# Seven-product order, standard parts ahead of the pair, and a late first gate chunk in a two-layer encoder

## The chip, the cores and the metric

The kernel runs on one core of one Trainium2 chip. The time is the device time of one execution in microseconds (us), the median of several runs. TensorE multiplies, VectorE and ScalarE work on tiles in SBUF and PSUM, GpSimd does a little, and SyncE issues the loads. In the rows PE is TensorE (PEld its weight loads), DVE is VectorE, ACT is ScalarE, POOL is GpSimd and SP is SyncE.

## What is computed

The reference is an encoder trunk over 256 positions of 2048 channels in f32, two layers deep. The change touches what stands at the end of each layer:

```
h = rms_norm(x, mlp_norm[i])
x = x + jnp.square(jax.nn.relu(h @ mlp_w1[i])) @ mlp_w2[i]      # 2048 -> 8192 -> 2048
g = jax.nn.sigmoid(rms_norm(x, ple_norm[i]) @ ple_w_gate[i])    # 2048 -> 2048
x = x + g * (p[i] @ ple_w_proj[i])
```

## The kernel before, in words

**Exact f32 from three passes.** Every operand of TensorE is held as two tiles, a high part (ScalarE's copy into fp32r) and a low part (VectorE's source minus high part). A product is three passes: high by high, high by low, low by high. So each weight tile of 128 x 2048 is loaded into one of four `raw` buffers (L86, DMA on SyncE), copied by ScalarE (L105) and subtracted by VectorE (L106) into one of four `hl` buffers. `Weights.run_ahead` (L118) issues loads and splits at most three tiles ahead of the one TensorE asks for with `ws.next()`; an `hl` buffer is free again when TensorE has used the tile four places earlier.

**The squared-ReLU mixer.** `mlp` (L556) goes over 16 blocks q of 512 hidden channels, two at a time (f = 0..7). `w1(q)` (L568) makes one block: four weight tiles, each 16 matmuls of 512 columns (L580) and 16 of 256 (L585), then ScalarE and VectorE turn the PSUM result into `h` and into four sums of its quarter blocks, `g`. `w2(f, n)` (L615) is a standard part: two weight tiles, 48 matmuls (L345), output columns n (512 of the 2048), added to x at L366. For the output columns n = 0 and 1 `pair(f)` (L621) uses seven products in place of eight for a matrix of 2 x 2 blocks: for each of the two blocks q of the pair seven products of six matmuls (L641). With x and y as the weight tiles of n = 0 and n = 1, each cut into a first and a second half (x0, xq, y0, yq), the products use: 1 x0, 2 xq, 3 yq, 5 x0 + y0, 6 x0 + y0 + yq, 7 y0 + yq, 4 x0 + y0 + yq + xq. VectorE makes the sums in place in the raw tile (L102), so a sum must come after the splits that read the old value, and the split after a sum needs it complete: first VectorE's sum, then ScalarE's copy, then VectorE's subtraction. `add_seven` (L69) puts two products into each `hl` tile: seven tiles for the two blocks of a pair.

**PSUM.** Three buffers of 1024 columns serve `w1`, `w2` and the pair's tiles a (products 1, 5), b (2, 3) and c (7, 6); tile d (product 4) is one of two buffers of 512 columns, which it shares with the transposes. After the second block, VectorE adds each finished tile to x or to `sums` (L649, L655, L657).

**The layer's order** (L674 to L690) is `w1(0)`, `w1(1)`, then for each f: `w1(2f+2)`, `w2(f,2)`, `pair(f)`, `w1(2f+3)`, `w2(f,3)`. At f = 7 there is no further `w1`; behind the pair stand `pair_end` (L659), which combines `sums` into x, and `w2(7,3)`. `after.chunk(c)` (L317) takes the squares of chunk c of x at once and puts its transposes, scaling and split off by four steps (`tick`). The gate that follows (`embed`, L692) multiplies chunks 0, 1, 2, 3 of the normed x by its weights.

**Who sets the order.** The instructions of TensorE and SyncE stand in the order of the program. Those of VectorE, ScalarE and GpSimd are ordered by the scheduler of the language; `tc.high_priority` moves some forward. Each engine then runs its list in order.

Of the kernel before, what the change touches and what calls it, by code (L numbers as in the profile page):

```python
# [15 lines left out]
ALU = mybir.AluOpType  # L16
# [14 lines left out]
RAW_BUFS = 4  # L31
RSQRT_MAGIC = float(0x5F3759DF)
# [10 lines left out]
class Weights:  # L43

# [24 lines left out]
    def add_seven(self, tiles):  # L69


        q, parts = 1024, []
        for x, y in tiles:
# [21 lines left out]
    def divide(self, after_first=None):  # L95
# [3 lines left out]
        for i, (what, (r, c), other, w) in enumerate(steps):  # L99
# [6 lines left out]
            getattr(self.nc, lo).tensor_tensor(hl[:, 1, to], src, hl[:, 0, to].bitcast(F32), ALU.subtract)  # L106
# [32 lines left out]
def encoder(ctx: ExitStack, tc: tile.TileContext, a, out: bass.AP):  # L139
# [35 lines left out]
    def add_mlp(i):  # L175
        def w1(q):
            for c in range(4):
                ws.add(a["mlp_w1"][i, q, c])
# [10 lines left out]
        for f in range(8):  # L189
            if f < 7:  # L190
                w1(2 * f + 2)
            w2(f, 2)
            pair(f)
            if f < 7:
                w1(2 * f + 3)
            w2(f, 3)
# [84 lines left out]
    class Norm:  # L281
# [35 lines left out]
        def chunk(self, c):  # L317
# [9 lines left out]
            put_off(lambda: self.scale(c, turned))  # L327
# [228 lines left out]
    def mlp(i, norm, after):  # L556
# [64 lines left out]
        def pair(f):  # L621


            p15, p76, p23 = psum_mm(f"ps_s{i}_{f}a"), None, psum_mm(f"ps_s{i}_{f}b")
            p4 = sm_pool.tile([P, 512], F32, tag="sm", name=f"ps_s{i}_{f}d")
            k = 0
            for q in (2 * f, 2 * f + 1):
                h, g = hidden[q], forms[q]
                for what in range(7):
                    if k % 2 == 0:  # L630
                        w = ws.next()
                    if what == 4 and p76 is None:
                        p76 = psum_mm(f"ps_s{i}_{f}c")
                    out_ps = (lambda: p15[:, :512], lambda: p23[:, :512], lambda: p23[:, 512:], lambda: p15[:, 512:],
                              lambda: p76[:, :512], lambda: p76[:, 512:], lambda: p4)[what]()
                    for kt in range(2):
                        for m, (s, j) in enumerate(PASSES_W_MOVES):
                            act = (h[:, s, kt, :P], h[:, s, 2 + kt, :P], g[:, s, 3, kt], g[:, s, 0, kt],
                                   g[:, s, 2, kt], g[:, s, 1, kt], h[:, s, 2 + kt, P:])[what]
                            col = (k % 2) * 1024 + kt * 512  # L640
                            nc.tensor.matmul(out_ps, lhsT=act, rhs=w[:, j, col:col + 512],  # L641
# [4 lines left out]
                    if q % 2 == 0:  # L646
                        continue
                    if what == 2:
                        nc.vector.tensor_tensor(x[:, 0, :1024], p23, x[:, 0, :1024], ALU.add)  # L649
                    elif what in (3, 5):  # L650
                        ps, to = (p15, sums[:, :1024]) if what == 3 else (p76, sums[:, 1024:])
                        if f == 0:
                            nc.scalar.activation(to, ps, AF.Copy)
                        else:
                            nc.vector.tensor_tensor(to, ps, to, ALU.add)  # L655
                    elif what == 6:
                        nc.vector.tensor_tensor(x[:, 1, :512], p4, x[:, 1, :512], ALU.add)  # L657

        def pair_end():  # L659
# [7 lines left out]
            after.chunk(0)  # L667
# [4 lines left out]
            after.chunk(1)  # L672
# [4 lines left out]
        for f in range(8):  # L677
# [3 lines left out]
            if f == 7:  # L681
                after.chunk(2)
            pair(f)
            if f == 7:
                pair_end()
            else:
                w1(2 * f + 3)
            w2(f, 3)
            if f == 7:
                after.chunk(3)  # L690
# [242 lines left out]
```

## Time and profile before

| | us |
|---|---|
| median of 3 runs (2074.29 to 2076.41) | 2075.16 |
| the profiled execution, its own time | 2070.65 |
| its span, first to last instruction | 2068.9 |
| PE busy | 1977.0 |
| DVE busy | 1564.3 |
| ACT busy | 1039.6 |

The profiled execution is a run of its own; its time is 1.75 us more than its span. Busy times are unions of instruction times, and those of TensorE overlap, so its busy share says little of how well it is fed. Whether it waits is read from the start times of its matmuls.

### The profile page before, as it was taken

The page shows a single profiled execution, that of the slowest core. Times are in us where ns is not written, and L with a number is a line of the kernel's source. Part 1 is how long each engine was busy: PE and PEld are TensorE (multiplying, and loading weights), DVE is VectorE, ACT ScalarE, POOL GpSimd, SP SyncE. Part 2 cuts the span into 40 slices and gives each one's busy share as a digit, 9 for nine tenths or more (in the row PEclk, how much of TensorE's full clock was granted, in tenths as well). Part 3 has the DMA queues.
Part 4 walks back from the last instruction along what each step waited for, and adds up shares of the span by engine and source line. Part 5 has one row for each costly group of instructions (what it writes and reads, how often), then busy time and mean ns, then how long its engine had stood idle before and what let it go on. Part 6 is the DMA issues. An engine that isn't in the chain of part 4 may idle for free.

```text
span 2068.9 us, 24040 instructions
## 1 busy us (share of the span) xinstructions
PE 1977.0 (96%) x9730; PEld 1668.3 (81%) x9730; DVE 1564.3 (76%) x1771; ACT 1039.6 (50%) x1087; POOL 128.9 (6%) x65
## 2 busy tenths in 40 slices
PE   8999999999999999998999999999999999999798
PEld 6888887878787787877789888787787878788686
DVE  7888768687787868779556567787868778787854
ACT  6345555445444545455454455545545445554543
POOL 3874000000000000000001000000000000000000
PEclk9999999999999999999999999999999999999999
DMA  8545554554536454464453554536364454635542
GB/s 330 192 170 191 206 188 168 187 203 143 224 140 227 152 214 183 143 223 162 152 183 135 183 183 146 224 139 240 137 231 169 159 209 146 222 135 203 182 164 108
DMA packets 55664, 377.43 MB, mean 182 GB/s; under 512 B 6384, under 2 KB 6528, under 8 KB 11648
## 3 DMA queue, kind: packets, MB, share of 16 engines
q1 hardware_dynamic: 55152, 374.82, 49.7%
q8 instruction: 76, 1.25, 0.2%
q10 hardware_dynamic: 144, 1.05, 0.1%
q14 instruction: 36, 0.29, 0.0%
q0 software_dynamic: 256, 0.02, 0.0%
HBM read 373.75 MB, written 2.10 MB: 182 GB/s over the span
## 4 chain that ended last, share of the span: by engine, by line
PE 69%; DVE 27%; issue 2%; ACT 2%; DMA 0%; ACTq 0%; SPq 0%
PE ps_h L580 21%; DVE hl L106 14%; PE ps_h L585 11%; PE ps_o L345 9%; PE ps_g L345 8%; DVE raw L102 7%; PE ps_od L345 4%; PE ps_in L345 4%; PE ps_out L345 3%; PE ps_pool L345 2%; ACT hl L105 2%; PE ps_outp L345 1%; PE ps_e L345 1%; DVE h L600 1%; DVE g L612 1%
## 5 line engine op out<-in xcount | busy, mean ns | idle before, releaser
L105 ACT ACTIVATE hl<-raw 128x2048 fp32r<-128x2048 f32 (+2 forms) x529 | 774.7, 1491 | 769.0 <-PE ps_h L585 315.8
L106 DVE TENSOR_TENSOR hl<-raw,hl 128x2048 fp32r<-128x2048 f32 (+3 forms) x501 | 865.5, 1744 | 381.5 <-ACT hl L105 379.8
L580 PE MATMUL ps_h<-xT_mlp,hl 128*128 128x512 f32 x2048 | 503.6, 399 | 0.0
L580 PEld LDWEIGHTS ps_h<-xT_mlp,hl 128*128 128x128 f32 x2048 | 391.1, 194 | 80.4
L345 PE MATMUL ps_o<-hl,h 128*128 128x512 f32 x1536 | 356.3, 391 | 0.0
L345 PEld LDWEIGHTS ps_o<-hl,h 128*128 128x128 f32 x1536 | 288.0, 189 | 58.7
L585 PEld LDWEIGHTS ps_h<-xT_mlp,hl 128*128 128x128 f32 x2048 | 262.6, 191 | 10.0
L585 PE MATMUL ps_h<-xT_mlp,hl 128*128 128x256 f32 x2048 | 266.0, 283 | 0.0
L345 PE MATMUL ps_g<-hl,xT_ple 128*128 128x512 f32 (+1 forms) x816 | 177.6, 377 | 0.0
L345 PEld LDWEIGHTS ps_g<-hl,xT_ple 128*128 128x128 f32 x816 | 146.4, 188 | 28.2 <-DVE hl L106 0.4
L106 POOL TENSOR_TENSOR hl<-raw,hl 128x2048 fp32r<-128x2048 f32 (+1 forms) x28 | 120.8, 4328 | 55.8 <-ACT hl L105 55.8
L345 PE MATMUL ps_in<-hl,xT_ev 128*128 128x512 f32 x384 | 90.8, 397 | 7.2 <-ACT hl L105 7.2
L442 DVE SCALAR_TENSOR_TENSOR acc<-vp,vT,acc 128x256 f32<-128x256 f32 x240 | 96.4, 481 | 0.1
L345 PEld LDWEIGHTS ps_in<-hl,xT_ev 128*128 128x128 f32 x384 | 73.4, 192 | 22.9 <-ACT hl L105 7.2
L345 PE MATMUL ps_od<-hl,f 128*128 128x512 f32 x384 | 88.1, 390 | 0.0
L595 ACT ACTIVATE relu<-ps_h 128x512 f32<-128x512 f32 x64 | 38.3, 598 | 96.4 <-PE ps_h L585 96.4
L345 PEld LDWEIGHTS ps_od<-hl,f 128*128 128x128 f32 x384 | 71.8, 188 | 14.8
L102 DVE TENSOR_TENSOR raw<-raw 128x1024 f32<-128x1024 f32 x64 | 78.0, 1219 | 0.7
L102 DVE TENSOR_TENSOR raw<-raw,raw 128x1024 f32<-128x1024 f32 x64 | 78.0, 1218 | 0.1
L782 POOL CAST top<-z 128x4 fp32r<-128x4 f32 x8 | 1.5, 189 | 931.7 <-DVE z L267 931.7
L596 DVE TENSOR_TENSOR relu<-ps_h,relu 128x512 f32<-128x512 f32 x64 | 42.7, 685 | 17.9 <-ACT relu L595 17.9
L611 ACT ACTIVATE g<-form 128x512 fp32r<-128x512 f32 x64 | 38.4, 623 | 24.4 <-DVE form L608 13.4
(283 smaller groups left out, 1716.6 us busy)
## 6 DMA issues: line engine op xcount, KB each, us to landing
raw<-in_mlp_w SPq DMA_DIRECT2D x256, 1024.0 KB, 4.9
raw<-in_ple_w_gate SPq DMA_DIRECT2D x32, 1024.0 KB, 5.0
raw<-in_w_in SPq DMA_DIRECT2D x20, 1024.0 KB, 5.0
raw<-in_ev_w_out SPq DMA_DIRECT2D x16, 1024.0 KB, 4.8
raw<-in_od_w_out SPq DMA_DIRECT2D x16, 1024.0 KB, 4.8
raw<-in_w_in SPq DMA_DIRECT2D x16, 256.0 KB, 6.3
raw<-in_ple_w_proj SPq DMA_DIRECT2D x8, 512.0 KB, 3.4
x<-in_x SPq DMA_DIRECT2D x2, 1024.0 KB, 7.9
```

The costliest lines, as they stand in the source:

```text
L102: self.nc.vector.tensor_tensor(src, src, self.raw[other[0]][:, other[1]:other[1] + w], ALU.add)
L105: self.nc.scalar.activation(hl[:, 0, to], src, AF.Copy)
L106: getattr(self.nc, lo).tensor_tensor(hl[:, 1, to], src, hl[:, 0, to].bitcast(F32), ALU.subtract)
L345: nc.tensor.matmul(ps[t][:, cols], lhsT=acts[:, s, kt, t * P:(t + 1) * P], rhs=w[:, m, kt * 512 + cols.start:kt * 512 + cols.stop], start= ...
L442: nc.vector.scalar_tensor_tensor(acc, src, cwT[:, ch, k:k + 1], acc, ALU.mult, ALU.add)
L580: nc.tensor.matmul(pss[p][:, e], lhsT=w[:, 0, ch], rhs=norm.xT[c][:, :, kt], start=c == 0 and kt == 0, stop=False, skip_group_check=True)
L585: nc.tensor.matmul(pss[p][:, e, 1], lhsT=w[:, 1, ch], rhs=norm.xT[c][:, 0, kt], start=False, stop=c == 3 and kt == 3, skip_group_check=True)
L595: nc.scalar.activation(r, pss[p][:, :, 1], AF.Copy)
L596: nc.vector.tensor_tensor(s, pss[p][:, :, 0], r, ALU.add)
L600: nc.vector.tensor_tensor(h[:, 1, e], s, h[:, 0, e].bitcast(F32), ALU.subtract)
L611: nc.scalar.activation(g[:, 0, to], src, AF.Copy)
L612: nc.vector.tensor_tensor(g[:, 1, to], src, g[:, 0, to].bitcast(F32), ALU.subtract)
```

## The change

1. **The order of the seven products** (`SEVEN`). Before, both blocks of a pair ran 1, 2, 3, 5, 7, 6, 4. Now the first runs 1, 2, 5, 3, 6, 7, 4 and the second 1, 5, 2, 6, 3, 4, 7. The sum that product 5 needs is made just ahead of 5, no longer ahead of 3. Number and size of splits, sums, matmuls and loads stay.
2. **Both standard parts first.** For f < 7 the order is now `w1(2f+2)`, `w2(f,2)`, `w2(f,3)`, `pair(f)`, `w1(2f+3)`, so `w1(2f+3)` and the next `w1(2f+4)` are neighbours. For f = 7: `w2(7,2)`, `pair(7)`, `w2(7,3)`. The weights are loaded and split in the new order.
3. **The end of the layer.** `pair_end` runs under high priority, chunk 0 is put off by 7 steps and chunk 1 by 9 (before 4 each), and the gate takes chunk 2 first, then 0, 1, 3.
4. **Without effect:** a branch for `lo == "dma"` in `divide`, which no caller asks for, and `lo="vector"` in `add_mlp`, which is the default.

```diff
+SEVEN = (1, 2, 5, 3, 6, 7, 4), (1, 5, 2, 6, 3, 4, 7)
...
-            parts += [
-                [("split", (x, 0))], [("split", (x, q))],
-                [("add", (x, 0), (y, 0)), ("split", (y, q))], [("split", (x, 0))],
-                [("add", (y, 0), (y, q)), ("split", (y, 0))], [("add", (x, 0), (y, q)), ("split", (x, 0))],
-                [("add", (x, 0), (x, q)), ("split", (x, 0))]]
+            made = {1: [("split", (x, 0))], 2: [("split", (x, q))], 3: [("split", (y, q))],
+                    5: [("add", (x, 0), (y, 0)), ("split", (x, 0))],
+                    6: [("add", (x, 0), (y, q)), ("split", (x, 0))],
+                    7: [("add", (y, 0), (y, q)), ("split", (y, 0))],
+                    4: [("add", (x, 0), (x, q)), ("split", (x, 0))]}
+            parts += [made[p] for p in SEVEN[k]]
...
-            parts = [(a["ple_w_gate"][i, n, c], 2048) for c in range(4)]
+            parts = [(a["ple_w_gate"][i, n, c], 2048) for c in (2, 0, 1, 3)]
...
-            put_off(lambda: self.scale(c, turned))
+            put_off(lambda: self.scale(c, turned), steps)
...
-            after.chunk(0)
+            after.chunk(0, 7)
...
-            after.chunk(1)
+            after.chunk(1, 9)
...
             w2(f, 2)
-            if f == 7:
-                after.chunk(2)
+            if f < 7:
+                w2(f, 3)
+                pair(f)
+                w1(2 * f + 3)
+                continue
+            after.chunk(2)
             pair(f)
-            if f == 7:
+            with tc.high_priority(offset=PRIO):
                 pair_end()
-            else:
-                w1(2 * f + 3)
             w2(f, 3)
-            if f == 7:
-                after.chunk(3)
+            after.chunk(3)
...
-                for c in range(4):
-                    rows_product(pg, norm.xT[c], range(4), c == 0, c == 3)
+                for k, c in enumerate((2, 0, 1, 3)):
+                    rows_product(pg, norm.xT[c], range(4), k == 0, k == 3)
```

**VectorE at the end of a pair** (f = 3 of the first layer). `raw` tiles are weights: 4519 and 4551 are x and y of the second block before, 4580 and 4612 are the same two now. Before, from the sum for product 6 on:

```order
L102 TENSOR_TENSOR raw_4519<-raw_4519,raw_4551 128x1024
L649 TENSOR_TENSOR x<-ps_s_3b,x 128x1024
L106 TENSOR_TENSOR hl_4648<-raw_4519,hl_4648 128x1024
L655 TENSOR_TENSOR sums<-ps_s_3a,sums 128x1024
L102 TENSOR_TENSOR raw_4519<-raw_4519 128x1024
L106 TENSOR_TENSOR hl_4669<-raw_4625,hl_4669 128x2048
L106 TENSOR_TENSOR hl_4648<-raw_4519,hl_4648 128x1024
```

Now, behind the addition of `w2(3,3)` to x at the pair's start and the split of the first block's product 4, the next twelve (L107 are sums, L115 the subtractions of the splits):

```order
L115 TENSOR_TENSOR hl_4647<-raw_4580,hl_4647 128x1024
L107 TENSOR_TENSOR raw_4580<-raw_4580,raw_4612 128x1024
L115 TENSOR_TENSOR hl_4667<-raw_4580,hl_4667 128x1024
L107 TENSOR_TENSOR raw_4612<-raw_4612 128x1024
L115 TENSOR_TENSOR hl_4667<-raw_4580,hl_4667 128x1024
L115 TENSOR_TENSOR hl_4687<-raw_4612,hl_4687 128x1024
L107 TENSOR_TENSOR raw_4580<-raw_4580,raw_4612 128x1024
L115 TENSOR_TENSOR hl_4687<-raw_4580,hl_4687 128x1024
L115 TENSOR_TENSOR hl_4708<-raw_4612,hl_4708 128x1024
L107 TENSOR_TENSOR raw_4580<-raw_4580 128x1024
L655 TENSOR_TENSOR sums<-ps_s_3a,sums 128x1024
L115 TENSOR_TENSOR hl_4708<-raw_4580,hl_4708 128x1024
```

Before, a split of the next `w1` (128x2048) stood ahead of the pair's last split, that of product 4; now that split stands ahead of all splits of the next `w1`, which follow behind the rows shown. Between the sum for product 4 and its split stands the addition of one finished tile (`sums`, tile a).

**TensorE at the end of the layer** (first layer). Before, from the second block's last two products on:

```order
L641 MATMUL ps_s_7d<-hl_6977,h_15_6735 128x512 x6
L345 MATMUL ps_o_7_3_7067<-hl_6998,h_14_6353 128x512 x24
L323 MATMUL tr_ple_00_7098<-ident,x 128x128 x4
L323 MATMUL tr_ple_01_7107<-ident,x 128x128 x4
L323 MATMUL tr_ple_10_7117<-ident,x 128x128 x4
L323 MATMUL tr_ple_11_7126<-ident,x 128x128 x4
L345 MATMUL ps_o_7_3_7067<-hl_7016,h_15_6735 128x512 x24
```

Now:

```order
L356 MATMUL ps_o_7_3_7067<-hl_6998,h_14_6353 128x512 x24
L356 MATMUL ps_o_7_3_7067<-hl_7016,h_15_6796 128x512 x18
L334 MATMUL tr_ple_00_7121<-ident,x 128x128 x4
L334 MATMUL tr_ple_01_7130<-ident,x 128x128 x4
L356 MATMUL ps_o_7_3_7067<-hl_7016,h_15_6796 128x512 x6
L356 MATMUL ps_g_0_7176<-hl_7034,xT_ple_2_6934 128x512 x6
L334 MATMUL tr_ple_10_7190<-ident,x 128x128 x4
L334 MATMUL tr_ple_11_7199<-ident,x 128x128 x4
L356 MATMUL ps_g_0_7176<-hl_7034,xT_ple_2_6934 128x512 x18
```

The transposes of chunk 0 (`tr_ple_0..`) move 18 matmuls later, those of chunk 1 behind the first six matmuls of the gate, which start on chunk 2.

**VectorE behind the last pair** (first layer), now:

```order
L115 TENSOR_TENSOR hl_6998<-raw_6953,hl_6998 128x2048
L115 TENSOR_TENSOR hl_7016<-raw_6974,hl_7016 128x2048
L647 TENSOR_TENSOR x<-ps_s_7b,x 128x1024
L649 TENSOR_TENSOR x<-ps_s_7d,x 128x512
L679 TENSOR_TENSOR x<-x,sums 128x512
L115 TENSOR_TENSOR hl_7034<-raw_6996,hl_7034 128x2048
L655 TENSOR_TENSOR sums<-ps_s_7c,sums 128x1024
L115 TENSOR_TENSOR hl_7070<-raw_7014,hl_7070 128x2048
L679 TENSOR_TENSOR sums<-sums 128x512
L115 TENSOR_TENSOR hl_7099<-raw_7032,hl_7099 128x2048
L679 TENSOR_TENSOR x<-x,sums 128x512
L679 TENSOR_TENSOR sums<-sums 128x512
```

L679 are the operations of `pair_end`; what chunk 0 needs of x is complete with the operation behind the last row shown. Three splits of gate weights (7034, 7070, 7099) still stand between them.

## Rows read from the trace of the kernel before

**Rows 1.** Head of the page.

```profile
span 2068.9 us, 24040 instructions
```

**Rows 2.** Stretches: one whole step f (510.87), and the last pair (949.14).

```profile
core 0: us, PE busy (x) PEld busy (x) DVE busy (x) ACT busy (x) POOL busy (x), PEclk, DMA share, GB/s
510.87:602.90 92.03, 88.52 (x437) 74.62 (x436) 71.71 (x67) 45.55 (x43) 0.00 (x0) 0.96 0.50 183
949.14:971.18 22.04, 20.50 (x94) 16.44 (x92) 21.54 (x21) 16.51 (x19) 0.00 (x0) 1.00 0.45 161
```

**Rows 3.** Stretches, a pair's first matmul to next w1's first L585.

```profile
330.63:356.76 26.13, 23.47 (x102) 18.61 (x100) 26.02 (x22) 17.13 (x15) 0.00 (x0) 1.00 0.51 190
602.90:632.32 29.42, 25.80 (x102) 20.25 (x100) 29.35 (x25) 16.21 (x13) 0.00 (x0) 0.88 0.55 203
...
sum 405.99, PE 356.87 PEld 280.86 DVE 404.13 ACT 229.57 POOL 0.00; mean PE 25.49 PEld 20.06 DVE 28.87 ACT 16.40 POOL 0.00
```

**Rows 4.** Timeline of PE in pair f = 3: start, length, count [idle before].

```profile
602.90 1.52 PE L641 MATMUL ps_s_3a<-hl,h 128*128 128x512 f32 x6
604.26 1.52 PE L641 MATMUL ps_s_3b<-hl,h 128*128 128x512 f32 x6
...
622.90 0.56 PE L641 MATMUL ps_s_3d<-hl,h 128*128 128x512 f32 x1 [1.92 <-ACT hl L105]
625.15 2.50 PE L641 MATMUL ps_s_3d<-hl,h 128*128 128x512 f32 x5 [1.69 <-DVE hl L106]
627.45 5.03 PE L580 MATMUL ps_h<-xT_mlp,hl 128*128 128x512 f32 x16
632.32 2.08 PE L585 MATMUL ps_h<-xT_mlp,hl 128*128 128x256 f32 x16
```

**Rows 5.** Chain that ended last, over the first two neighbouring w1: start, length, what.

```profile
292.05 3.65 PE ps_h L580 x16
...
297.62 3.65 PE ps_h L580 x16
```

**Rows 6.** Timeline from the last pair into the gate, first layer.

```profile
977.05 0.68 DVE L662 TENSOR_TENSOR x<-x,sums 128x512 f32<-128x512 f32 x1
977.78 0.33 PE L323 MATMUL tr_ple<-ident,x 128*128 128x128 f32 x1 [1.00 <-DVE x L662]
982.39 1.76 PE L323 MATMUL tr_ple<-ident,x 128*128 128x128 f32 x7 [4.28 <-DVE x L662]
988.18 1.94 PE L323 MATMUL tr_ple<-ident,x 128*128 128x128 f32 x8 [4.04 <-DVE xT_ple L267]
...
1001.76 1.03 PE L323 MATMUL tr_ple<-ident,x 128*128 128x128 f32 x8
1002.55 0.71 PE L345 MATMUL ps_g<-hl,xT_ple 128*128 128x512 f32 x2
```

**Rows 7.** Timeline of the last pair, f = 7, first layer.

```profile
949.14 1.52 PE L641 MATMUL ps_s_7a<-hl,h 128*128 128x512 f32 x6
949.34 1.29 DVE L366 TENSOR_TENSOR x<-ps_o,x 128x512 f32<-128x512 f32 x2 [0.45 <-PE ps_o L345]
...
959.21 1.62 PE L641 MATMUL ps_s_7d<-hl,h 128*128 128x512 f32 x6 [0.84 <-DVE xT_ple L267]
...
969.92 1.43 PE L641 MATMUL ps_s_7d<-hl,h 128*128 128x512 f32 x5 [0.70 <-DVE hl L106]
```

**Rows 8.** Timeline of DVE and ACT in pair f = 3.

```profile
610.08 1.22 DVE L102 TENSOR_TENSOR raw<-raw,raw 128x1024 f32<-128x1024 f32 x1
...
612.35 1.22 DVE L102 TENSOR_TENSOR raw<-raw 128x1024 f32<-128x1024 f32 x1
...
613.60 1.06 ACT L105 ACTIVATE hl<-raw 128x1024 fp32r<-128x1024 f32 x1 [1.15 <-DVE raw L102]
...
620.54 1.22 DVE L102 TENSOR_TENSOR raw<-raw 128x1024 f32<-128x1024 f32 x1
...
631.15 2.28 DVE L106 TENSOR_TENSOR hl<-raw,hl 128x2048 fp32r<-128x2048 f32 x1
```

More of the change, by code (lines that the diff above doesn't have):

```diff
@@ L177, in w1 @@
             for c in range(4):
-                ws.add(a["mlp_w1"][i, q, c])
+                ws.add(a["mlp_w1"][i, q, c], lo="vector")
         def w2(f, n):
@@ L315, in scale, with chunk @@
                     divide_psum((xt[:, 0, 2 * h + j], xt[:, 1, 2 * h + j]), s[:, j], vT[:, k:k + 1])
-        def chunk(self, c):
+        def chunk(self, c, steps=4):
             def turned(h):
@@ L621, in pair, with psum, gather @@
         def pair(f):
-            p15, p76, p23 = psum_mm(f"ps_s{i}_{f}a"), None, psum_mm(f"ps_s{i}_{f}b")
-            p4 = sm_pool.tile([P, 512], F32, tag="sm", name=f"ps_s{i}_{f}d")
+            tiles = {}
+            def psum(p):
+                key, half = {1: ("a", 0), 5: ("a", 1), 2: ("b", 0), 3: ("b", 1), 7: ("c", 0), 6: ("c", 1), 4: ("d", 0)}[p]
+                if key not in tiles:
+                    name = f"ps_s{i}_{f}{key}"
+                    tiles[key] = sm_pool.tile([P, 512], F32, tag="sm", name=name) if key == "d" else psum_mm(name)
+                return tiles[key][:, half * 512:(half + 1) * 512]
+            def gather(p):
+                if p == 3:
+                    nc.vector.tensor_tensor(x[:, 0, :1024], tiles["b"], x[:, 0, :1024], ALU.add)
+                elif p == 4:
+                    nc.vector.tensor_tensor(x[:, 1, :512], tiles["d"], x[:, 1, :512], ALU.add)
+                elif p in (5, 7):
+                    ps, to = (tiles["a"], sums[:, :1024]) if p == 5 else (tiles["c"], sums[:, 1024:])
+                    if f == 0:
+                        nc.scalar.activation(to, ps, AF.Copy)
+                    else:
+                        nc.vector.tensor_tensor(to, ps, to, ALU.add)
             k = 0
@@ L628, in pair @@
                 h, g = hidden[q], forms[q]
[L629 removed]
+                for p in SEVEN[q % 2]:
                     if k % 2 == 0:
                         w = ws.next()
[L632 to L635, printed above, removed]
                     for kt in range(2):
                         for m, (s, j) in enumerate(PASSES_W_MOVES):
[L638 to L639 removed]
+                            act = {1: h[:, s, kt, :P], 2: h[:, s, 2 + kt, :P], 4: h[:, s, 2 + kt, P:], 5: g[:, s, 0, kt],
+                                   6: g[:, s, 1, kt], 7: g[:, s, 2, kt], 3: g[:, s, 3, kt]}[p]
                             col = (k % 2) * 1024 + kt * 512
[L641 removed]
+                            nc.tensor.matmul(psum(p), lhsT=act, rhs=w[:, j, col:col + 512],
                                              start=q % 2 == 0 and kt == 0 and m == 0,
@@ L645, in pair @@
                     k += 1
[L646 to L653, printed above, removed]
-                        else:
-                            nc.vector.tensor_tensor(to, ps, to, ALU.add)
-                    elif what == 6:
-                        nc.vector.tensor_tensor(x[:, 1, :512], p4, x[:, 1, :512], ALU.add)
+                    if q % 2:
+                        gather(p)
         def pair_end():
@@ L731, in embed @@
             else:
-                for c in range(4):
-                    rows_product(pg, norm.xT[c], range(4), c == 0, c == 3)
+                for k, c in enumerate((2, 0, 1, 3)):
+                    rows_product(pg, norm.xT[c], range(4), k == 0, k == 3)
                 rows_product(pe, pT, range(2), True, True)
```

21 lines of the change are left out of this document (13 added, 8 removed).

## The prediction

> **What bounds the kernel now.** I read the views in this order: the head of the page, the stretches, the timeline of one step f, and the timeline from the last pair into the gate. The head gives a span of 2068.9 us [rows 1]. Over one whole step f, VectorE works 71.7 of 92.0 us and ScalarE 45.6 [rows 2], so no engine besides TensorE is full on average. Inside a pair it is otherwise: from the pair's first matmul VectorE is busy for 29.35 of 29.42 us [rows 3], and TensorE runs dry near the end. A product of six matmuls takes 1.36 us (602.90 to 604.26), yet the last product starts its first matmul after 1.92 us of idling for ScalarE's high part, and its second after 1.69 us for VectorE's low part [rows 4]. What the waits do to TensorE's clock stands beside them. The next matmuls come every 0.43 us (625.15 to 627.45 for five), which is the 1.2 GHz level, and the following 16 wide ones take 4.87 us (627.45 to 632.32) [rows 4] where an undisturbed 16 take 3.65 [rows 5]. The granted clock over the stretch is 0.88, while the first pair, with a wait as well, kept 1.00 [rows 3]. So a pair pays for the wait and, usually, for the clock.
>
> The sum over the 14 pairs f = 0 to 6 of both layers is 405.99 us [rows 3]. Fed without a wait, each would take 14 x 1.36 + 3.65 = 22.69 us [rows 4, 5], together 317.7. **88.3 us are lost there**, 6.3 a pair. The second loss is the end of the layer, where TensorE's transposes wait 1.00, 4.28 and 4.04 us for VectorE [rows 6].
>
> **The change, part by part.** The sum is made against the profiled execution, 2070.65 us, which is 4.5 us below the median of the runs, 2075.16; the gain is then taken off the median. Matmuls, splits, sums, additions and bytes loaded keep their number and size, so nothing is added or removed but waits.
>
> *Pairs 0 to 6.* With both standard parts ahead of it, a pair has 21.8 us of TensorE work, not 10.9, in which VectorE makes the relu's operations and the splits and sums of the first block. The last pair has that arrangement today (`w2(6,3)` and `w2(7,2)` stand between `w1(15)` and it), and its clock stayed at 1.00 [rows 2]. What is left is VectorE's list behind the pair's start, which the order gives. It starts 0.20 us after the first matmul (949.14 to 949.34) with two additions of 1.29 us [rows 7], at 1.5. Then come eight operations of 1024 columns up to the sum for product 6. Nine such operations in a row took 10.46 us today (610.08 to 620.54), 1.16 each [rows 8], so that sum ends at 10.8. The next split needs ScalarE's copy of the sum. The copy began 0.03 us after VectorE's sum was done (612.35 + 1.22 to 613.60) and took 1.06 [rows 8]; with the way back I count 1.14 us of idling, to 11.9. Two splits and the sum for product 4 lead to 15.4. Another 1.14 for its copy (the addition of tile a fits within it) leads to 16.5, and the split's 1.22 to 17.8. TensorE would want this low part at its second matmul of the seventh tile, 6 x 2.72 + 0.23 = 16.55. So it still waits about 1.25 us, and 0.13 are lost on the matmuls behind a wait of this size (969.92 to 971.18 for five, 1.26 us where 1.13 are due) [rows 2, 7]. **1.4 us a pair remain**, 19.6 in all; the gain is 88.3 - 19.6 = **68.7 us**. Bounds for the remainder: 0.8 a pair, as if only the last pair's 0.70 and its 0.13 were left [rows 7], and 3.4, what the first pair loses today at full clock (26.13 - 22.69) [rows 3]. I take 1.4, which is nearer to the last pair's row, whose arrangement it copies.
>
> What could be late next is covered. The splits of the following `w1` move behind the pair's last split, but its first 16 matmuls (3.65 us) need the high part alone, and the low part's 2.28 us [rows 4, 8] end before those do. SyncE loads the tiles in the new order; the second block's raw tiles are asked for one standard part earlier than today, and the first tile of the next `w1` can load as soon as the first block's product 4 is split. The two `w1` that are now neighbours share a PSUM tile that ScalarE and VectorE must first empty. Neighbours stand at the start of each layer today, and the wide matmuls follow across their border as within a block (292.05 to 297.62, 5.57 us, of which 3.65 are the 16 wide ones) [rows 5]: I take nothing for it; at worst it waits for one split on either engine, some 2 us at 12 borders.
>
> *The last pair* gives one standard part away and is entered as pairs 1 to 6 are today. Tile d waits for both transposed halves of chunk 2 to leave PSUM, 0.84 us today [rows 7]. VectorE reaches that point later by about 0.7 (1.55 in place of 0.84); its last split and the first of `w2(7,3)` cost 0.4 and 0.6. That makes 2.6 us in place of the 2.2 of now (22.04 - 14 x 1.36 - 0.79 for eight transposes, 1001.76 to 1002.55) [rows 2, 6]: a loss of 0.4 a layer.
>
> *The end of the layer.* Today from 971.18 [rows 2] to the gate's first chunk and its transposes (1002.55) 31.4 us pass [rows 6]; 72 matmuls of 0.227 and 24 transposes need 18.7. 12.7 are lost. In the new list VectorE must do five splits of 2.28, two additions of 1.22 and six operations of 0.68 [rows 6, 8] between the pair's last split (some 20.4 us after its start: the walk above, the split of product 7 and chunk 2's part in between) and the value that chunk 0's transposes need: 17.9 us, to 38.3. TensorE arrives there 32.0 us after the pair's start (21.9 for the pair with its transposes and waits, 0.6, and 42 matmuls). It waits some 6 us, not the 1.00 and 4.28 of now. Chunk 1's second half then waits for chunk 0's to leave PSUM, behind a split of 2.28 and the addition to x: about 4 us, like the 4.04 of now. With 0.8 for smaller waits and 1 for the clock this is 11.8, a gain of 0.9 a layer. Later steps and the high priority thus bring little: the queue in front of them is as long as the time they give. Bounds: 5 us more or 3 us less a layer. Chunk 2 first in the gate hides nothing further; its operand is long there.
>
> Sum: 68.7 + 2 x (0.9 - 0.4) = 69.7 us. The profiled execution would be 2001.0, **the median 2005.5**. The pairs' bounds move it by -8 and +28, the layers' ends by -10 and +6; by the remainder that I hold likely (0.8 to 2.4) it lies between 1991 and 2024.
>
> **The rivals.**
> - *A second wait in the pair* (9 in 100). The sum for product 6 and its copy come late too, since ScalarE's list holds the copies behind one that waits for a sum. For it: today's pairs wait for high part and low part in turn [rows 4]. Against it: product 6's split has half a microsecond in hand. With 3.4 us a pair: 14 x 2.0 = 28 us less gain, 2033.5.
> - *The clock still falls* (9 in 100). A wait of 1.25 us lies between the last pair's 0.70, after which the clock was 1.00 [rows 2, 7], and the 3.6 with one matmul between, after which it was 0.88 [rows 3, 4]. If it falls, each pair pays up to 2.2 more (five matmuls 1.0 late, sixteen 1.2 late) [rows 4]: 14 x 2.2 = 31, 2036. The Trainium skill, TensorE: Matmul & The Clock Gate, Part 1, says that the throttled state is the default and that activity releases it, so that idling brings it back. The pairs f = 1 to 6 agree with that; the first pair, at 1.00 after its own wait, does not show it.
> - *No change* (3 in 100). VectorE has as much to do as before and was full in the pair; then the wait only moves elsewhere, and the time stays at 2075. The Trainium skill, Perfetto Trace Analysis, section Identifying the Most-Contended Engine, takes VectorE's occupancy as a fair measure of its nearness to its limit; by it a pair at 29.35 of 29.42 [rows 3] could gain nothing by order alone. The 20 us in which VectorE is idle in each step [rows 2] speak against it, since half of the first block's work can go there.
> - *Slower* (4 in 100): every split waits out its ScalarE copy. If all eight splits of 1024 columns behind the pair's start stood 1.14 us behind their copies, not two, the remainder would grow by 6.8 to 8.2, with the clock's 2.2 to 10.4, 4.1 over today's 6.3: 14 x 4.1 = 57 us slower, 2132. It decides from the fifth late copy on. Against it: the copies of products 2, 3 and 7 need no sum that is fresh.
> - *All pairs fed* (9 in 100). The copies overlap better than counted and nothing waits: 88.3 and 1, 1986.
>
> **How the numbers follow.** The forecast has 66 in 100, with 1991 to 2024 as its own range. Adding the two rivals that end at 2033.5 and 2036 gives 84; the range **1990 to 2036** leaves out the upside beyond it, no change and slower. About 0.2% (4 us) is what a measurement of this kernel can tell. Faster by more has 66 + 9 + 9 + 9 = 93 in 100, no difference 3, slower 4.
>
> **What would show it.** In the profile after, a stretch from a pair's first matmul to the next `w1`'s first matmul of 256 columns takes about 24.1 us at a clock of 1.00, a step f about 87 us, and the one wait left stands ahead of tile d in the seventh tile and ends with VectorE. The transposes of chunk 0 wait about 6 us, those of chunk 1 about 4. I am wrong on the pair if its stretches stay above 26 us, on the clock if they show 0.88 with a short wait, on the layer's end if its waits sum to under 5 us, and on the whole if waits appear inside `w1` or the standard parts.

## The result, and the profile after

The kernel after takes **2002.2 us** (median of 4 runs, 2001.22 to 2002.58) against 2074.72 for the kernel before in the same comparison. The ratio is 0.9653, with a 95% interval of 0.9636 to 0.967. The forecast was 2005.5 in a range of 1990 to 2036. The profiled execution took 2001.22 us, with a span of 1999.4, where 2001.0 was forecast. VectorE and ScalarE are busy as long as before (1566.5 and 1041.2 us); what went is waiting of TensorE, and matmuls that ran slowly behind the waits.

The stretches of the pairs after, from a pair's first matmul to the next `w1`'s first matmul of 256 columns, with the columns of [rows 2]:

```profile
342.91:366.90 23.99, 23.23 (x101) 18.69 (x100) 21.50 (x18) 16.64 (x14) 0.00 (x0) 1.00 0.54 197
...
602.88:626.85 23.97, 23.20 (x101) 18.69 (x100) 22.61 (x19) 14.88 (x12) 0.00 (x0) 1.00 0.53 196
...
sum 335.69, PE 325.03 PEld 261.70 DVE 314.39 ACT 210.69 POOL 0.00; mean PE 23.22 PEld 18.69 DVE 22.46 ACT 15.05 POOL 0.00
```

They answer to [rows 3]: 335.69 us where 405.99 stood, so 70.3 are gained. All fourteen lie between 23.96 and 24.01, and all at a granted clock of 1.00 (the 2.4 GHz level). VectorE is still busy for 94% of a pair (22.61 of 23.97), but the pair waits less for it.

The timeline of TensorE in pair f = 3 after, from product 4 of the second block on (start, length, engine, line, what, count, idle time before), answers to [rows 4]:

```profile
619.34 0.49 PE L668 MATMUL ps_s_3d<-hl,h 128*128 128x512 f32 x1
620.60 1.43 PE L668 MATMUL ps_s_3d<-hl,h 128*128 128x512 f32 x5 [0.77 <-DVE hl L115]
621.87 1.52 PE L668 MATMUL ps_s_3c<-hl,g 128*128 128x512 f32 x6
623.23 3.79 PE L591 MATMUL ps_h<-xT_mlp,hl 128*128 128x512 f32 x16
```

The two waits of 1.92 and 1.69 us are one, in the place that was named. The row says 0.77, counted from the end of a matmul; from start to start the second matmul comes 1.03 us late (620.60 - 619.34 - 0.23). Of the 5.45 us that this pair gained (29.42 to 23.97) some 2.3 are the clock's: the five matmuls behind the wait take 1.27 us where they took 2.30, and the sixteen of `w1` 3.62 (623.23 to 626.85) where they took 4.87.

The timeline of VectorE in the same pair:

```profile
603.09 1.29 DVE L377 TENSOR_TENSOR x<-ps_o,x 128x512 f32<-128x512 f32 x2 [0.57 <-PE ps_o L356]
...
606.67 1.23 DVE L107 TENSOR_TENSOR raw<-raw,raw 128x1024 f32<-128x1024 f32 x1
...
612.36 1.22 DVE L107 TENSOR_TENSOR raw<-raw,raw 128x1024 f32<-128x1024 f32 x1
614.70 2.36 DVE L115 TENSOR_TENSOR hl<-raw,hl 128x1024 fp32r<-128x1024 f32 x2 [1.12 <-ACT hl L110]
616.98 1.22 DVE L107 TENSOR_TENSOR raw<-raw 128x1024 f32<-128x1024 f32 x1
618.11 1.21 DVE L655 TENSOR_TENSOR sums<-ps_s_3a,sums 128x1024 f32<-128x1024 f32 x1
619.32 1.23 DVE L115 TENSOR_TENSOR hl<-raw,hl 128x1024 fp32r<-128x1024 f32 x1
```

This is the walk of the prediction, step for step: the start 0.21 us behind TensorE's, the sum for product 6 done at 10.7 us (10.8 forecast), 1.12 of idling for its copy (1.14), the last split done at 17.67 (17.8).

The end of the first layer after, TensorE's rows with waits, answers to [rows 6, 7]:

```profile
926.72 1.62 PE L668 MATMUL ps_s_7d<-hl,h 128*128 128x512 f32 x6 [1.22 <-DVE xT_ple L278]
...
938.77 9.63 PE L356 MATMUL ps_o<-hl,h 128*128 128x512 f32 x41 [0.32 <-DVE hl L115]
948.24 0.27 PE L334 MATMUL tr_ple<-ident,x 128*128 128x128 f32 x1
953.45 1.76 PE L334 MATMUL tr_ple<-ident,x 128*128 128x128 f32 x7 [4.94 <-DVE x L679]
954.86 2.91 PE L356 MATMUL ps_o<-hl,h 128*128 128x512 f32 x6
957.56 2.13 PE L356 MATMUL ps_g<-hl,xT_ple 128*128 128x512 f32 x6
...
962.58 1.09 PE L334 MATMUL tr_ple<-ident,x 128*128 128x128 f32 x4 [2.46 <-DVE tot_ple L314]
```

The pattern of before (1.00, 4.28, 4.04) has become one wait of 4.94 for chunk 0 and one of 2.46 for chunk 1. Behind the first the clock is at its lower level: six matmuls of `w2(7,3)` take 2.70 us (954.86 to 957.56), 0.45 each. In the second layer the waits lie elsewhere (4.97 for chunk 0, 0.47 and 0.84 for chunk 1, 1.18 and 1.45 for chunk 3) and come to the same: from the last pair's start to the end of chunk 3's transposes 53.14 and 53.19 us pass in the two layers, 53.41 before in both.

Where the rest of the time went is read from stretches outside the pairs. Before: from the end of pair 6 to the first pair of the second layer, from the end of its pair 6 to the program's end, and from the start to the first pair:

```profile
908.74:1291.43 382.69, 371.83 (x1886) 316.80 (x1884) 252.27 (x287) 192.27 (x234) 6.24 (x20) 0.99 0.47 169
1871.29:2068.90 197.61, 176.60 (x853) 148.22 (x851) 129.69 (x164) 90.19 (x112) 0.00 (x0) 0.96 0.43 158
0.00:330.63 330.63, 319.76 (x1562) 269.94 (x1563) 267.07 (x486) 174.69 (x209) 122.65 (x45) 1.00 0.56 204
```

The same three after:

```profile
886.75:1269.13 382.38, 373.38 (x1885) 317.68 (x1884) 258.43 (x292) 193.95 (x235) 6.24 (x20) 0.99 0.48 172
1812.98:1999.40 186.42, 165.78 (x805) 138.38 (x803) 127.36 (x163) 87.25 (x111) 0.00 (x0) 0.96 0.44 162
0.00:342.91 342.91, 331.85 (x1610) 279.00 (x1611) 276.95 (x492) 179.30 (x211) 122.61 (x45) 1.00 0.56 203
```

A standard part of 48 matmuls (10.9 us) has moved from the end of the second layer to the start of the first. With that taken into account the two layer ends gave 0.3 us each, and the part ahead of the first pair, in which little was changed, took 1.4 us longer. (In the four kernels of the next section that part takes between 330.4 and 332.4 us, less the standard part where it stands there, so 1.4 is no more than what it varies by.) Together: 70.3 + 0.3 + 0.3 - 1.4 = 69.5, which is the difference of the spans (2068.9 - 1999.4). Outside the pair a whole step f takes what it took (92.03 - 29.37 before, 86.63 - 23.97 after, both 62.66; about 87 was forecast for the step), so the neighbouring `w1` cost nothing, as the prediction took it.

### The profile page after: what moved, and what is told of

Same layout as the page of the kernel before. It is cut to its first block, busy times and chain, and to the rows that moved or that the text cites. A ratio compares the mean times of both kernels' runs of the same rounds, so it can differ in the third digit from the quotient of the medians.

```text
span 1999.4 us, 24088 instructions
## 1 busy us (share of the span) xinstructions
PE 1948.0 (97%) x9730; PEld 1649.4 (82%) x9730; DVE 1566.5 (78%) x1771; ACT 1041.2 (52%) x1087; POOL 128.8 (6%) x65
## 4 chain that ended last, share of the span: by engine, by line
PE 80%; DVE 17%; ACT 1%; issue 1%; DMA 0%; SPq 0%; ACTq 0%
PE ps_h L591 23%; PE ps_o L356 16%; PE ps_h L596 12%; DVE hl L115 9%; PE ps_g L356 8%; PE ps_od L356 4%; DVE raw L107 4%; PE ps_in L356 4%; PE ps_out L356 3%; PE ps_pool L356 2%; ACT hl L110 1%; PE ps_outp L356 1%; PE ps_e L356 1%; DVE sums L655 1%; DVE x L377 1%
## 5 line engine op out<-in xcount | busy, mean ns | idle before, releaser
L110 ACT ACTIVATE hl<-raw 128x1024 fp32r<-128x1024 f32 (+2 forms) x529 | 775.5, 1491 | 689.2 <-PE ps_h L596 244.1
L115 DVE TENSOR_TENSOR hl<-raw,hl 128x2048 fp32r<-128x2048 f32 (+3 forms) x501 | 861.7, 1743 | 298.4 <-ACT hl L110 296.9
L591 PE MATMUL ps_h<-xT_mlp,hl 128*128 128x512 f32 x2048 | 488.2, 390 | 0.0
L591 PEld LDWEIGHTS ps_h<-xT_mlp,hl 128*128 128x128 f32 x2048 | 377.4, 188 | 73.7
L596 PEld LDWEIGHTS ps_h<-xT_mlp,hl 128*128 128x128 f32 x2048 | 262.6, 191 | 9.9
L115 POOL TENSOR_TENSOR hl<-raw,hl 128x2048 fp32r<-128x2048 f32 (+1 forms) x28 | 120.7, 4325 | 57.3 <-ACT hl L110 57.3
L107 DVE TENSOR_TENSOR raw<-raw,raw 128x1024 f32<-128x1024 f32 x64 | 77.9, 1218 | 0.5
L107 DVE TENSOR_TENSOR raw<-raw 128x1024 f32<-128x1024 f32 x64 | 77.7, 1217 | 0.1
```

The lines of the kernel that those rows point to most:

```text
L107: self.nc.vector.tensor_tensor(src, src, self.raw[other[0]][:, other[1]:other[1] + w], ALU.add)
L110: self.nc.scalar.activation(hl[:, 0, to], src, AF.Copy)
L591: nc.tensor.matmul(pss[p][:, e], lhsT=w[:, 0, ch], rhs=norm.xT[c][:, :, kt], start=c == 0 and kt == 0, stop=False, skip_group_check=True)
L596: nc.tensor.matmul(pss[p][:, e, 1], lhsT=w[:, 1, ch], rhs=norm.xT[c][:, 0, kt], start=False, stop=c == 3 and kt == 3, skip_group_check=True)
```

## The experiments

The theory (A): a pair ends when VectorE has worked off its list, counted from the pair's start, and the end of a layer waits for splits of gate weights that VectorE has ahead of `pair_end`. Rivals: ScalarE's copies set the end; one part of the change does all; the clock alone.

### One part at a time

**The order of products alone** (`e1_order`):

```diff
+SEVEN = (1, 2, 5, 3, 6, 7, 4), (1, 5, 2, 6, 3, 4, 7)
...
+            parts += [made[p] for p in SEVEN[k]]
...
```

> The kernel before with the new order of the seven products alone: one standard part ahead of the pair and one behind, old end of the layer. Theory A (the end of a pair is set by VectorE's list behind the pair's start): VectorE still enters the pair behind the relu of the w1 before and with a split of the first block in hand, so it reaches the split for product 4 some 21 to 22 us after the pair's first matmul, where TensorE asks for it at 16.55. The wait is 4 to 5 us, about as long as before (3.6) but now at one place, and the clock falls or stays; a pair takes 27 to 29.5 us (before 29.0 on average, after 23.98). The time is 2055 to 2080. Theory B (it is ScalarE's copies that the last splits wait for, and the order spreads them): the order alone gives most of the gain, pairs near 25 us, 2015 to 2025.

**The standard parts alone** (`e2_parts`):

```diff
             w2(f, 2)
...
+            if f < 7:
+                w2(f, 3)
+                pair(f)
+                w1(2 * f + 3)
+                continue
...
```

> The kernel before with both standard parts ahead of the pair alone: old order of the seven products, old end of the layer. Theory A: VectorE has done the first block's splits by the pair's start, and 2 additions of 1.29 us, 13 operations of some 1.16 and a split of the next w1 (2.28) lead to the split for product 4 at 19 to 20 us, where TensorE asks for it at 16.55. 2.5 to 3.5 us of waiting a pair are left, with or without 2 for the clock: pairs of 25.5 to 28 us, gain 14 to 48 of the 72 us, 2027 to 2061. Theory B (the place of the parts alone sets it): pairs near 24 us as in the kernel after, 2005. Theory C (the order alone does it): pairs stay near 29, 2075.

**The layer's end alone** (`e3_end`):

```diff
-                pair_end()
+                with tc.high_priority(offset=PRIO):
+                    pair_end()
...
+            after.chunk(0, 7)
+            after.chunk(1, 9)
...
+                for k, c in enumerate((2, 0, 1, 3)):
...
```

> The kernel before with the changed end of the layer alone: pair_end under high priority, chunk 0 put off by 7 steps and chunk 1 by 9, the gate takes chunk 2 first. Theory A (the waits there are set by splits of gate weights that stand ahead of pair_end on VectorE): the two waits of 4 us keep their sum, at other places, 2071 to 2079. Theory B (the later transposes give TensorE work to cover VectorE's delay): each layer gains 3 to 4 us, 2067 to 2069.

**The kernel after with the old end** (`e4_no_end`), the reverse of the edit above:

> The kernel after with the old end of the layer (pair_end without priority, both chunks put off by 4 steps, gate in order 0, 1, 2, 3), so the product order and the standard parts together. Theory A: all of the gain lies in the pairs, 2000 to 2006. Theory B (the new end gives 3 to 4 us a layer that the last pair eats): 2008 to 2011. The 14 pair stretches are 23.98 us in both.

Measured:

| kernel | median us | ratio to before, interval | sum of the 14 pairs |
|---|---|---|---|
| order alone | 2052.33 | 0.9893 (0.9876 to 0.9909) | 386.41 |
| parts alone | 2010.36 | 0.9694 (0.968 to 0.9709) | 338.11 |
| end alone | 2066.49 | 0.996 (0.9946 to 0.9973) | 409.89 |
| order and parts | 2004.28 | 0.9666 (0.9652 to 0.968) | 335.70 |
| all three (after) | 2002.2 | 0.9653 (0.9636 to 0.967) | 335.69 |

The place of the standard parts does nearly all: 67.9 of the 70.3 us in the pairs. The order alone gives 19.6, but on top of the parts only 2.4. So the parts alone came out near the 2005 of the rival, and the order alone a little under theory A's 2055 (its pairs take 27.6 us on average). For the parts alone theory A had counted 2.5 to 3.5 us of waiting a pair; it is 1.0:

```profile
616.20 2.29 DVE L106 TENSOR_TENSOR hl<-raw,hl 128x2048 fp32r<-128x2048 f32 x1
```

```profile
619.57 0.39 PE L643 MATMUL ps_s_3d<-hl,h 128*128 128x512 f32 x1
620.81 1.43 PE L643 MATMUL ps_s_3d<-hl,h 128*128 128x512 f32 x5 [0.85 <-DVE hl L106]
```

The error was in the deadline. In the old order product 4 is the fourteenth product and not the thirteenth, so TensorE asks for its low part at 17.9 us and not at 16.55. VectorE had it at 18.9 (620.81, the pair starts at 601.89), behind a split of the next `w1` (2.29 us). The new order takes that split out of the way and brings the deadline 1.36 us forward; the two nearly cancel. In pair f = 3 of the four kernels TensorE gets this low part 22.25 us after the pair's start before, 20.60 with the order alone, 18.92 with the parts alone and 17.72 after; it asks for it at 17.91 in the old order and at 16.55 in the new, later by what it waited earlier in the pair.

With the order alone TensorE waits at two places in each pair, twice at each, and the same waits meet two clocks. Two neighbouring pairs, f = 3 and 4 of the first layer:

```profile
602.92:631.46 28.54, 25.54 (x101) 19.73 (x100) 27.89 (x24) 15.48 (x12) 0.00 (x0) 0.94 0.55 201
694.13:720.98 26.85, 23.84 (x102) 18.61 (x101) 26.19 (x22) 14.94 (x12) 0.00 (x0) 1.00 0.52 187
```

The waits are 0.30, 0.76, 0.52 and 1.42 us in the one and 0.30, 0.76, 0.53 and 1.42 in the other; after those of the first the clock fell, after those of the second it stayed, a difference of 1.7 us. The rival of the clock thus had a price of the right kind (2.2 us forecast), but not the condition: whether the clock falls is not decided by the length of the waits alone. Nor is the clock alone the cause of what a pair loses: the second of these pairs takes 26.85 us at 1.00, the first pair of before 26.13, the pairs of after 23.97.

The end alone went against theory A: 7.1 us gained, not none, a little more than theory B's 3 to 4 a layer. In its profiled execution the two layer ends take 376.01 and 195.81 us where 382.69 and 197.61 stood. Its pairs, which the edit leaves alone, take 3.9 us more than before (409.89 and 405.99): in some of them the clock is lower (the first takes 28.82 us at 0.88, where it took 26.13 at 1.00), so with unfed pairs the sum varies by that much. With only two gate splits ahead of chunk 0's value on VectorE (three in the kernel after), TensorE's 42 matmuls of `w2(7,3)` cover most of VectorE's delay:

```profile
988.00 0.98 PE L323 MATMUL tr_ple<-ident,x 128*128 128x128 f32 x7 [1.41 <-DVE x L662]
...
994.05 1.94 PE L323 MATMUL tr_ple<-ident,x 128*128 128x128 f32 x8 [2.32 <-DVE xT_ple L267]
```

On top of the other parts the same edit gives 2.1 us between the medians (2004.28 to 2002.2), which two separate comparisons can hardly tell apart: the intervals of their ratios overlap. The profiled executions show it better. The two layer ends with order and parts alone:

```profile
885.18:1270.26 385.08, 372.85 (x1886) 317.14 (x1885) 258.63 (x292) 194.47 (x235) 6.26 (x20) 0.98 0.47 171
1814.10:2003.00 188.90, 166.51 (x805) 139.41 (x803) 127.44 (x163) 88.11 (x111) 0.00 (x0) 0.94 0.43 160
```

In the kernel after they take 382.38 and 186.42, so 2.7 and 2.5 us less. Against before (382.69, and 197.61 less the standard part's 10.9) order and parts with the old end lose 2.4 and 2.2 us there, and the new end wins that back. It wins less than alone: a third split has come ahead of the sums by then, as the rows of VectorE below show.

### What an operation on VectorE's list is worth in a pair

**A low part made twice** (`e10_dup`):

```diff
+                      "twice" if k == 6 else "vector")
...
-                getattr(self.nc, lo).tensor_tensor(hl[:, 1, to], src, hl[:, 0, to].bitcast(F32), ALU.subtract)
+                for _ in range(2 if lo == "twice" and other == 0 else 1):
+                    self.nc.vector.tensor_tensor(hl[:, 1, to], src, hl[:, 0, to].bitcast(F32), ALU.subtract)
```

> The kernel after with VectorE's low part of the first block's product 4 made twice in each pair (same value to the same place, so the output stays). VectorE's list becomes 1.14 us longer. Theory A: the wait ahead of the last product 4 grows from 1.03 to some 2.2 us in each of 14 pairs (and in the last pair): 16 to 18 us more if the clock stays at 1.00, 2018 to 2021, and up to 2.2 us a pair beyond that if it falls, 2050. Theory B (VectorE has slack behind ScalarE's copies): under 5 us more.

It took 2100.59 us, but this time can't be read as the price: the edit names VectorE for every split, and so also moved the first part's GpSimd splits to VectorE. TensorE waited 22.2 and 15.9 us for them in two groups of products there, long before the pairs. The pairs can be read on their own: they sum to 372.29 us, 36.6 more than after or 2.6 each, more than the 1.14 that was added. Most of the other 1.5 comes from two sums of PSUM tiles that the scheduler had put ahead of the late splits, where they waited for TensorE (0.74 and 0.63 us); in three of the 14 pairs the clock fell to 0.94 as well:

```profile
681.17 1.23 DVE L657 TENSOR_TENSOR sums<-ps_s_3a,sums 128x1024 f32<-128x1024 f32 x1 [0.74 <-PE ps_s_3a L670]
...
686.43 1.23 DVE L649 TENSOR_TENSOR x<-ps_s_3b,x 128x1024 f32<-128x1024 f32 x1 [0.63 <-PE ps_s_3b L670]
```

VectorE has no slack there (the rival's 5 us are excluded), but the exact price stays open here.

**One low part on GpSimd** (`e7_pair_pool`):

```diff
-                       for i, part in enumerate(parts[k:k + 2]) for step in part])
+                       for i, part in enumerate(parts[k:k + 2]) for step in part],
+                      ("gpsimd", "vector") if k == 6 else "vector")
...
```

> The kernel after with one low part of 1024 columns of each pair (the first block's product 4, the first that VectorE makes within the pair) on GpSimd. VectorE's list in the pair becomes 1.16 us shorter; sums and ScalarE's copies stay. Theory A (VectorE's list ends the pair): the wait of 1.03 us ahead of the last product 4 goes, pairs take 22.7 to 22.9 us in place of 23.98, 15 to 18 us less, 1984 to 1987. Theory B (the trip sum, ScalarE's copy, VectorE's subtraction or ScalarE's own list sets it): the wait stays within 0.3 us, 1998 to 2003.

2019.58 us (0.973, 0.9715 to 0.9744): slower than after, which neither theory had. The rows of GpSimd and VectorE in pair f = 3 say why:

```profile
607.99 2.40 POOL L117 TENSOR_TENSOR hl<-raw,hl 128x1024 fp32r<-128x1024 f32 x1 [85.31 <-ACT hl L111]
```

```profile
608.89 2.59 DVE L117 TENSOR_TENSOR hl<-raw,hl 128x1024 fp32r<-128x1024 f32 x1 [0.76 <-ACT hl L111]
611.51 1.22 DVE L108 TENSOR_TENSOR raw<-raw,raw 128x1024 f32<-128x1024 f32 x1
```

VectorE's split began while GpSimd was at work and took 2.59 us in place of 1.22; it ended 1.09 us after GpSimd's did, as if it had stood until then. Its next sum starts 4.86 us after the pair's start (606.65), in the kernel after 3.79: the list is 1.07 us later, not 1.16 earlier. The longer split (1.37 us more) is not the whole miss. VectorE waits 0.76 us for ScalarE's copy ahead of it, a wait that the split taken away had covered: it starts 2.24 us after the pair's start, and 2.54 in the kernel after. So even at 1.22 us the list would have been only 0.3 us shorter, and the forecast's 15 to 18 us would not have come. The pairs sum to 351.18, so 1.11 us more each. A microsecond on VectorE's list was a microsecond of the pair here. The Trainium skill, Perfetto Trace Analysis, section Optimizing Scalar/DVE Operations, warns that GpSimd and VectorE share a read port of SBUF and that moving work between them may not help; the trace agrees, with 2.59 for 1.22.

**One low part by DMA** (`e12_pair_dma`, with the kernel's own unused branch: ScalarE writes minus the high part, a DMA adds the weights):

```diff
+                      ("vector", "dma") if k == 8 else "vector")
...
```

> The kernel after with one low part of 1024 columns of each pair (the second block's product 2) made by ScalarE (1.06 us more) and an accumulating DMA. VectorE's list in the pair becomes 1.13 us shorter, and nothing runs on GpSimd beside it. Theory A (VectorE's list from the pair's start ends the pair): the wait of 1.03 us ahead of product 4 goes, pairs take 22.7 to 23.0 us in place of 23.98, 14 to 18 us less, 1984 to 1988. Theory B (ScalarE's copies set it): pairs stay at 24.0 or grow by ScalarE's 1.06, 2002 to 2018.

1984.5 us (0.9565, 0.9549 to 0.9581), as theory A has it:

```profile
615.42 1.23 DVE L117 TENSOR_TENSOR hl<-raw,hl 128x1024 fp32r<-128x1024 f32 x1
```

```profile
616.31 1.82 PE L670 MATMUL ps_s_3d<-hl,h 128*128 128x512 f32 x6
```

The last split starts 15.43 us after the pair's start (599.99) where it was 16.44, and the six matmuls of product 4 stand in one row. They are still 0.3 us late (1.66 us to the next product's start at 617.97, where 1.36 are due). The pairs sum to 321.90, 13.8 less than after, 22.99 each where 22.69 would be fed. ScalarE had 1.06 us more to do in each and cost nothing, which ends the rival that its copies limit the pair; the two trips from sum to copy to split stay in VectorE's list.

### What stands ahead of the sums at the layer's end

VectorE in the kernel after, behind the last pair:

```profile
943.17 2.28 DVE L115 TENSOR_TENSOR hl<-raw,hl 128x2048 fp32r<-128x2048 f32 x1
945.37 1.21 DVE L655 TENSOR_TENSOR sums<-ps_s_7c,sums 128x1024 f32<-128x1024 f32 x1
946.50 2.28 DVE L115 TENSOR_TENSOR hl<-raw,hl 128x2048 fp32r<-128x2048 f32 x1
...
949.31 2.28 DVE L115 TENSOR_TENSOR hl<-raw,hl 128x2048 fp32r<-128x2048 f32 x1
...
952.71 2.61 DVE L679 TENSOR_TENSOR x<-x,sums 128x512 f32<-128x512 f32 x4
```

Three splits of gate weights (2.28 each) stand between the sums; TensorE is ready from 948.24 on.

**Their low parts on GpSimd** (`e6_gate_pool`), and **together with the pair's** (`e8_both_pool`):

```diff
-            for src, cols in parts:
-                ws.add(src, cols=cols)
+            for k, (src, cols) in enumerate(parts):
+                ws.add(src, cols=cols, lo="gpsimd" if n == 0 and k < 3 else "vector")
```

> The kernel after with the low parts of the first three gate weight tiles of each layer (chunks 2, 0 and 1) made on GpSimd in place of VectorE; a low part of 2048 columns takes 4.33 us there (GpSimd's splits in the first part of the trace of before). In the kernel after, three such splits (2.28 us each) stand between the last pair's sums and the value that chunk 0's transposes wait 5.14 us for. Theory A (those splits make the wait): the wait goes, and the clock after it stays up; each layer gains 5 to 8 us, 1986 to 1992. Theory B (the wait is for something else, such as the additions of the last product's PSUM tiles): under 1 us a layer, 2000 to 2003.

> The two edits before this one together. Theory A: the gains add, 1969 to 1976, faster than both kernels. Theory B: no more than the better of the two.

2014.79 and 2034.16 us, both worse than after. VectorE is held up more still: beside GpSimd's split of 4.61 us from 943.21 on, VectorE's addition, which takes 0.68 elsewhere, took 5.01:

```profile
943.35 5.01 DVE L679 TENSOR_TENSOR x<-x,sums 128x512 f32<-128x512 f32 x1
```

So these two runs say nothing on the question they were made for.

**By DMA** (`e11_gate_dma`: `"dma"` where `"gpsimd"` stands above), and **together with the pair's** (`e13_both_dma`):

> The kernel after with the low parts of the first three gate weight tiles of each layer made without VectorE and GpSimd's arithmetic: ScalarE writes minus the high part (some 1.9 us each more for ScalarE), and an accumulating DMA adds the weights from memory (the branch lo == 'dma' of the kernel). It repeats the test that the GpSimd version could not make, since there GpSimd's subtractions stretched VectorE's. Theory A (three splits of 2.28 us ahead of the sums make the wait of 5.14 us ahead of chunk 0's transposes): the wait falls by 4.5 us or goes, and the rows behind it run at full clock; 5 to 8 us a layer, 1986 to 1993. Theory B (the wait has another cause): within 2 us of the kernel after, 2000 to 2004. If the DMA itself comes late, a new wait stands ahead of the gate's low products.

> The two edits before this one together. Theory A: the gains add, 1970 to 1980, faster than both kernels. Theory B: within 3 us of the better of the two.

2002.27 and 1985.07 us: no gain over their bases, and yet the wait of 4.94 us is gone:

```profile
949.55 1.03 PE L334 MATMUL tr_ple<-ident,x 128*128 128x128 f32 x8
...
951.81 0.39 PE L356 MATMUL ps_g<-hl,xT_ple 128*128 128x512 f32 x1
958.91 2.50 PE L356 MATMUL ps_g<-hl,xT_ple 128*128 128x512 f32 x5 [6.71 <-DMA hl<-in_ple_w_gate]
```

The transposes run as soon as TensorE gets there, so the splits did make the wait. A new one took its place, for the first tile's DMA: three DMAs of 1 MB beside the loads of the gate landed 15.8 us after their issue (median).

**Only the second and third tile by DMA**, with the pair's (`e14_late_dma`):

```diff
...
+                ws.add(src, cols=cols, lo="dma" if n == 0 and k in (1, 2) else "vector")
```

> The kernel with product 2's low part of each pair by DMA (1984.5 us), and with the low parts of the gate's second and third weight tiles by DMA as well, while the first, which the gate needs at once, stays on VectorE. With all three by DMA the transposes no longer waited (5.14 us to none), but the gate's first low part came 6.7 us late. Theory A (VectorE's splits ahead of pair_end make the transposes' wait, and the second and third tile's DMAs have time enough): two splits of 2.28 less are ahead of the sums, the wait of 4.04 us goes, the clock stays at full speed behind it, and each layer gains 4 to 7 us: 1970 to 1977. Theory B (the DMAs, at 1 MB each beside the loads of the gate, come late again): a wait ahead of the gate's second or third tile takes the place, 1981 to 1987.

**1978.56 us** (0.9534, 0.9519 to 0.955; runs 1976.82 to 1979.84), the fastest version, faster than both kernels, and between the two forecasts (1970 to 1977, 1981 to 1987). In the first layer the transposes of chunks 0 and 1 run without a wait, as theory A has it; those of chunk 3 wait 0.81 and 1.64 us:

```profile
942.21 1.03 PE L336 MATMUL tr_ple<-ident,x 128*128 128x128 f32 x8
...
951.91 0.63 PE L336 MATMUL tr_ple<-ident,x 128*128 128x128 f32 x4 [0.81 <-DVE rstd_ple L287]
954.19 1.09 PE L336 MATMUL tr_ple<-ident,x 128*128 128x128 f32 x4 [1.64 <-DVE rs_q L291]
```

The second layer is not as it has it. The transposes of chunks 0 and 1 are on time there too, but chunk 3's wait 7.82 us:

```profile
1871.44 1.94 PE L336 MATMUL tr_ple<-ident,x 128*128 128x128 f32 x8 [7.82 <-DVE xT_ple L280]
```

ScalarE's rows show the load of the final norm's weights, which ScalarE itself issues:

```profile
1857.21 5.15 ACTq L842 DMA_DIRECT2D gfin<-in_final_norm  x1
...
1862.47 0.63 ACT L310 ACTIVATE junk<-x 128x512 bf16<-128x512 f32 x1 [4.25 <-issue]
```

The issue took 5.15 us (0.37 in the kernel after), and ScalarE stood for 4.25, and VectorE 4.41 for ScalarE. How much of the 7.82 comes from that is not shown: issuing the load elsewhere wasn't tried.

## Why the prediction was right, and where not

- **The pairs**: 70.3 us gained, 68.7 forecast; 1.28 us lost a pair, 1.4 forecast; the one wait left is where it was named, and the walk to it holds step by step. The mechanism is shown by taking one operation off VectorE's list (1.0 us less a pair) and by delaying the list by 1.07 us (1.11 more).
- **The share of the two edits** was not separated in the prediction. The runs put 67.9 us to the place of the standard parts alone. Of the order, on which most of the walk was spent, 2.4 depend. The total doesn't suffer from it, since the walk counts both edits together.
- **The clock** stayed at 1.00 in all fourteen pairs, so that rival is out for this kernel; the order alone shows that waits of up to 1.4 us can bring it down in one pair and not in the next.
- **The last pair**: tile d waits 1.22 us by the row and starts 1.38 late, 1.55 forecast; the last split costs 0.36, 0.4 forecast, and the first of `w2(7,3)` 0.48, 0.6 forecast.
- **The layer's end** gave 0.3 us a layer with the last pair, 0.5 forecast. Its terms were less exact than the sum. In the first layer VectorE had chunk 0's value 37.1 us after the pair's start (38.3 forecast) and TensorE was there at 32.0 as forecast; chunk 0's transposes came 5.1 us late (6 forecast) and chunk 1's 2.7 (4). The clock, put at 1 us, cost some 4: 2.6 behind the first wait (953.45 to 959.53, 6.1 us for work of 3.5) and 1.5 behind the second. The step that failed is "Later steps and the high priority thus bring little". They bring 2.7 and 2.5 us in the two layers on top of the other edits, and 7.1 us alone. That the net is small has another reason, which the prediction had too small: with the old end the other two edits cost the layer's end 2.4 and 2.2 us, where it counted 0.4 a layer for the last pair. The two errors cancel in the sum.
- **No change, slower**: neither came. VectorE's work is what it was, and its busy share in the pair is still 94%; the share did not say what the order was worth. No wait came up inside `w1` or the standard parts ahead of the pairs.
- **All pairs fed** (1986) was not reached by the change. One operation less on VectorE comes to that time (1984.5), though its pairs still lose 0.3 us each.
- **From profile to median**: the profiled execution of before lay 4.5 us under its median, that of after 1.0 under its own. That the sum for the profile was right within 0.3 us is partly luck: its terms missed by up to 1.6 and cancelled (pairs +1.6, ends -0.4, first part -1.4). How the range of 1991 to 2024 comes from its bounds the prediction does not show; the likely remainders (0.8 to 2.4) and the ends' bounds, added up, give 1987 to 2026.

## What to carry to other kernels

An engine that is full within a stretch but idle around it can be a matter of order: count its list from the start of the stretch, operation by operation with the waits for partners, against the moment at which the next engine asks for the last result. Find that moment for each order anew, since moving the asking product by one place was worth as much here as the operation taken out of its way. Parts of a change that work on the same wait don't add. And an operation taken off the list brings only what the waits for partners behind it leave: one split of 1.13 us brought 1.0 at one place of the pair, and by the rows would have brought 0.3 at another.

## What was not expected of the hardware

- GpSimd's subtractions held up what VectorE did beside them: a split took 2.59 us for 1.22, an addition 5.01 for 0.68. A DMA that GpSimd issued did not: with it VectorE's operations in the pair kept 1.22 us, and an accumulating DMA of 512 KB landed in 5.6 us (median).
- After the same four waits the clock stood at 0.94 over one pair and at 1.00 over the next.
- A DMA issue on ScalarE's own queue can hold its arithmetic for 4.25 us where the same issue took 0.37 in the kernel after. Two accumulating DMAs of 1 MB (14.7 us to landing, median) and loads of the gate's weights were under way; which of them it waited for stays open.
